# Encoder trunk on one core: x added group by group, scales and sinks loaded in the first network, two activation buffers asked for later, two norm buffers for four blocks

## Chip, cores, metric

The kernel runs on one core of one Trainium2 chip. The metric is the device time of one execution in microseconds (us), taken as the median of several runs. One profiled execution gives the trace from which all lines below come; times in it are counted from the start of its span.

## What is computed

Two layers (DEPTH = 2) of an encoder over 512 tokens of width 1024, each with four sublayers, all in float32, and each ended by a layer norm over the sum with its input:

```python
ALPHA = (2.0 * DEPTH) ** 0.25
for i in range(DEPTH):
    j = i // 2
    y = swiglu(x, ffn_w_gate[i, 0], ffn_w_up[i, 0], ffn_w_down[i, 0])
    x = layer_norm(ALPHA * x + 0.5 * y, ln_g[i, 0], ln_b[i, 0])
    if i % 2 == 0:
        y = mixer_ab(x, ab_w_in[j], ab_w_out[j], ab_q_gain[j], ab_k_gain[j], ab_sink[j], ang_2d, ang_1d)
    else:
        y = mixer_c(x, c_w_in[j], c_w_out[j], c_rpb[j])
    x = layer_norm(ALPHA * x + y, ln_g[i, 1], ln_b[i, 1])
    y = memory_attn(x, mem, mem_w_q[i], mem_w_kv[i], mem_w_o[i])
    x = layer_norm(ALPHA * x + y, ln_g[i, 2], ln_b[i, 2])
    y = swiglu(x, ffn_w_gate[i, 1], ffn_w_up[i, 1], ffn_w_down[i, 1])
    x = layer_norm(ALPHA * x + 0.5 * y, ln_g[i, 3], ln_b[i, 3])
```

`swiglu` is `(silu(x @ w_gate) * (x @ w_up)) @ w_down` with 2816 hidden features. In `mixer_ab`, q and k of the A heads are RMS-normed with a learned scale (`ab_q_gain`, `ab_k_gain`, 64 numbers each) before a rotary embedding, and the B heads have one learned sink logit each (`ab_sink`).

## The kernel before

**Stages.** `run` calls eight stages in order: network 0 (`ffn(0)`), `mixer_ab`, `memory(0)`, networks 1 and 2 (`ffn(1)`, `ffn(2)`), `mixer_c`, `memory(1)`, network 3. The 512 tokens lie in four blocks of 128 rows, `self.x[0]` to `self.x[3]`, each [128, 1024]; the same values transposed and split in two float32r parts are `xh` and `xl`. Every matmul is three products of such parts (`mm3`): high by high, high by low, low by high. So each weight is loaded, its high half is made by a cast on ScalarE (ACT) and its low half by a subtraction on VectorE (DVE); that is `split`.

**A network.** `ffn` works in groups of 512 hidden features. Group 0 is done plainly: 256 features by `ffn_by_features` (network 0) or `ffn_by_tokens` (the others), 256 by `hidden`. Groups 1 to 4 (`hidden_steps`, `down_steps`) use Strassen's seven products. In group g the steps of the hidden layer of g are interleaved with the steps of the down projection of group g-1, 28 steps in all, and `pipeline` loads for a step three steps ahead and splits its weights one step ahead. The down products come in the order (1, 6, 2, 5, 3, 7, 4), each for two token blocks b; products 2 and 3 add into blocks 0 and 1, products 5, 7 and 4 into blocks 2 and 3, on VectorE. Some sums of weights are made by a second load that adds onto the first (`plus`, an accumulating DMA on POOL's queue). The last 256 features come at the end (`finish`), block by block, with the norm of each block.

In network 0 the first down products write the x tiles instead of adding to them, and the input x itself is added by an accumulating DMA of 512 KB per block on POOL's queue (`add_x`). All four are asked for after group 1, in `after_first`, where the masks (`band`, `near`) are loaded too.

**The norm.** `layer_norm(t, ...)` has sums of the rows from the last additions; VectorE makes the negative mean `nmu` and `y = (x + nmu) * g`, ScalarE the sum of squares (`var`, written beside `junk`), POOL the reciprocal root in two operations (`rsqrt`, tile `lny`), VectorE the end, `x = y * r + b`. Then TensorE transposes the block and `split` makes `xh` and `xl`.

**The first mixer's start.** `mixer_ab` loads three rotary tables, `rope_2d` twice and `rope_1d`, into slabs, and the scales of q into the tile `gain` by three DMAs, and POOL multiplies the q table by them in four operations. The scales of k go through the same tile (one buffer) into the k table. The sinks are loaded after that and negated on VectorE. All these loads are on SP's queue, behind the last load of the network (`nc.after`).

**Buffers.** Weights, their halves, activations, norm buffers, `ln_g` and `ln_b` share one pool of 27 slabs of 4 KB per partition. `raw` has two buffers of 8 KB. PSUM has banks a (3), d (2), t (3).

**The order.** Nothing is run when it is written down: `Graph` records all operations with their dependencies, and `emit` plans each engine's order at build time with its own costs (`cost`) and issues them so. An operation is ready when what it depends on is done and its buffers are granted. Among the ready ones of an engine the one that was recorded first goes first, with a short patience on VectorE and ScalarE. A pool's buffers are granted strictly in the order in which they were asked for, whichever is used first. On the chip each engine then works in that fixed order, and a waiting instruction holds up all behind it. All recorded instructions carry line 143.

The central lines of the buffers' order:

```python
        def grant(space):

            while space.next < len(space.queue) and space.free:
                info = space.queue[space.next]
                space.next += 1
```

Of the kernel before, what the change touches and what calls it, by code (L numbers as in the profile page):

```python
# [17 lines left out]
ALU = mybir.AluOpType  # L18
# [234 lines left out]
class Kernel:  # L253
# [118 lines left out]
    def rsqrt(self, sums, n, tag, mean, eps):  # L372

        nc = self.nc
        y = self.small(n, tag + "y")
        nc.gpsimd.tensor_scalar(y, sums, mean, eps, ALU.mult, ALU.add)
        nc.gpsimd.tensor_tensor(out=y, in0=y, in1=self.nhalf[:, :n], op=ALU.pow)
        return y
# [32 lines left out]
    def layer_norm(self, t, st, gb, last):  # L411

        nc = self.nc
        g, b = gb
        x = self.x[t]
        halves = [(0, 512), (512, D)] if last and t == NT - 1 else [(0, D)]
        nmu = self.small(1, "nmu")
        nc.vector.tensor_scalar(nmu, st[:, 0:1], st[:, 1:2], -1.0 / D, ALU.add, ALU.mult)
        var = self.small(1, "var")
        y = self.slab(F32)  # L420
# [19 lines left out]
    def down(self, acts, wts, coef, ln=None, blocks=range(NT)):  # L440
# [3 lines left out]
        for t in blocks:  # L444
            st = self.small(2, "st") if ln else None
# [41 lines left out]
    def ffn_by_features(self, wg, wu, dst):  # L487
# [9 lines left out]
        for lo, hi in steps:  # L497
# [10 lines left out]
            for k in range(lo, hi):  # L508
                for parts, pair in zip(got, banks):
                    for b, ps in enumerate(pair):  # L510
                        st = [z[:, k % 4, b * P : (b + 1) * P] for z in parts[k // 4]]
                        self.mm3(ps, st, self.xT(k, 0, S), k == 0, k == KB - 1)
        for b in range(2):
            self.gated(banks[0][b], banks[1][b], dst=dst[:, :, b, :])

    def ffn_by_tokens(self, wg, wu, dst):
# [3 lines left out]
        for t in range(NT):  # L520
# [7 lines left out]
            sgs.append(self.gated(*both, 256))  # L528
        for b in range(2):
            ps = self.transposed([(t * P, P, sgs[t][:, b * P : (b + 1) * P]) for t in range(NT)])  # L530
            self.nc.scalar.copy(dst[:, :, b, :], ps.rearrange("p (s n) -> p s n", s=2))

# [22 lines left out]
    def hidden(self, wg, wu, c0, dst=None):  # L555

        gate, up = self.w_halves(wg, c0), self.w_halves(wu, c0)
        got = []
        for b in range(2):
# [4 lines left out]
            got.append(self.gated(pg, pu, dst=None if dst is None else dst[:, :, b, :]))  # L564
        return got
# [194 lines left out]
    def ffn(self, i, ln_i, last, aside=None):  # L760
# [8 lines left out]
        hs[0].extend(self.slab(F32, (P, 2, 2, 256)) for _ in range(2))  # L769
        if i == 0:  # L770
            self.ffn_by_features(wg, wu, hs[0][0])
        else:
            self.ffn_by_tokens(wg, wu, hs[0][0])
        self.hidden(wg, wu, groups[0][1], hs[0][1])
        xs = self.token_sums()

        def after_first():
            if i == 0:
                for t in range(NT):
                    self.add_x(t)  # L780
            if aside:
                nc.after = [op for op in nc.ops if op.dma and op.engine == "sync"][-1], {"sync"}
                aside()
                nc.after = None

        steps = []
        for g in range(1, 5):
# [5 lines left out]
            if g == 1:  # L793
                steps.append(only(after_first))
        tail, wt, ln, ws = [], {}, {}, []
# [109 lines left out]
    def mixer_ab(self, ln_i, last):  # L905
# [14 lines left out]
        for name, gain in (("q", "ab_q_gain"), ("k", "ab_k_gain"), ("b", None)):  # L920
# [5 lines left out]
            if gain:  # L926
                gn = self.small(128, "gain", 1)
                nc.sync.dma_start(out=gn[:, 0:64], in_=a[gain][0:1, :].broadcast_to([P, 64]))
                for h in range(2):
                    nc.sync.dma_start(  # L930
                        out=gn[:, 64 + 32 * h : 96 + 32 * h],
                        in_=a[gain][0:1, 32 - 32 * h : 64 - 32 * h].broadcast_to([P, 32]),
                    )
                for t in range(NT):
                    nc.gpsimd.tensor_tensor(out=tab[:, t, :], in0=tab[:, t, :], in1=gn, op=ALU.mult)
            tabs[name] = tab
        nsink = self.small(8, "nsink", 1)
        nc.sync.dma_start(out=nsink, in_=a["ab_sink"][0:1, :].broadcast_to([P, 8]))
        nc.vector.tensor_scalar(nsink, nsink, -1.0, None, ALU.mult)
# [487 lines left out]
    def masks(self):  # L1427
# [3 lines left out]
        self.nc.sync.dma_start(out=self.near, in_=self.a["near"])  # L1431

# [99 lines left out]
```

## Time and profile before

| | us |
|---|---|
| median of 3 runs (lowest, highest) | 2179.78 (2179.76, 2180.21) |
| the profiled execution | 2181.09 |
| its span, first to last instruction | 2179.3 |

The mean granted TensorE clock is 0.993 of full speed. DMA queues moved 273.89 MB; 13.3% of the 16 DMA engines' time went to the software queue (POOL's), 32.8% to the hardware queue (SP's and ACT's).

A line of a timeline has the start, the length of the merged piece, the engine, the operation, out<-in by tile names, the count, and in brackets the engine's idle time before it and what ended that. A line of the chain of waits has start, length, what. PE is TensorE's matmul, PEld its weight load, SPq the sequencer of SP, which issues most loads. A row on DMA issues has the tile, the queue, the count, KB each and the median time from issue to landing.

### The profile page before, as it was taken

What the parts mean: (1) busy time and instruction counts of PE and PEld (TensorE: products, weight loads), DVE (VectorE), ACT (ScalarE), POOL (GpSimd) and SP (SyncE); (2) the same over time, 40 slices, a digit from 0 to 9 for tenths busy, and PEclk for the clock granted to TensorE, in tenths of its full rate; (3) what the DMA queues carried; (4) which work ended last, traced back from release to release, by engine and by line L of the source; (5) the groups of instructions that cost most, each with busy time, mean ns of one, the idle gap of its engine ahead of it and who ended that gap; (6) DMA issues with size and microseconds to landing.
All of it is one profiled execution on the core that took longest, in us unless ns stands there. A gap on an engine that the chain in (4) does not pass through costs nothing.

```text
span 2179.3 us, 33960 instructions
## 1 busy us (share of the span) xinstructions
PE 2135.5 (98%) x13408; PEld 1923.0 (88%) x13408; DVE 1726.6 (79%) x2461; ACT 1066.8 (49%) x1671; POOL 350.6 (16%) x467
## 2 busy tenths in 40 slices
PE   9999999999999999999999999999999999999997
PEld 7989987778898899999789999888989989999996
DVE  7789987788755868999778999867677558699996
ACT  5545443467443544545435455445554435445552
POOL 0010013544000000000200001304330000000002
PEclk9999999999999999999999999999999999999999
DMA  6665552102442346556335555545553423465552
GB/s 194 165 144 138 141 180 73 32 11 70 134 135 88 97 116 179 142 136 164 107 82 141 146 135 141 155 117 149 147 164 117 135 88 98 116 148 146 134 155 67
DMA packets 210575, 273.89 MB, mean 126 GB/s; under 512 B 10481, under 2 KB 159601, under 8 KB 210417
## 3 DMA queue, kind: packets, MB, share of 16 engines
q1 hardware_dynamic: 178704, 221.14, 32.8%
q0 software_dynamic: 31424, 50.34, 13.3%
q8 instruction: 105, 1.72, 0.3%
q14 instruction: 54, 0.43, 0.1%
q10 hardware_dynamic: 288, 0.26, 0.0%
HBM read 257.02 MB, written 4.19 MB: 120 GB/s over the span
## 4 chain that ended last, share of the span: by engine, by line
PE 91%; DVE 3%; DMA 2%; ACT 1%; POOL 1%; issue 1%; SPq 1%; DVEq 0%; POOLq 0%; ACTq 0%
PE a L143 56%; PE d L143 21%; PE t L143 13%; DVE slab L143 2%; DVE x L143 1%; DVE t L143 1%; ACT slab L143 1%; POOL slab L143 1%; SPq L143 1%; DMA slab<-ffn_w_down 0%; DMA slab<-ffn_w_up 0%; DMA raw<-ab_w_out 0%; ACT t L143 0%; DMA gain<-ab_k_gain 0%; ACT junk L143 0%
## 5 line engine op out<-in xcount | busy, mean ns | idle before, releaser
L143 DVE TENSOR_TENSOR slab<-slab,slab 128x1024 fp32r<-128x1024 f32 (+3 forms) x614 | 696.9, 1163 | 50.0 <-ACT slab L143 27.2
L143 ACT CAST slab<-slab 128x1024 fp32r<-128x1024 f32 (+2 forms) x478 | 456.8, 984 | 322.9 <-DVE slab L143 138.6
L143 PE MATMUL a<-slab,slab 128*128 128x256 f32 (+3 forms) x2744 | 590.6, 307 | 2.4 <-ACT t L143 1.1
L143 PE MATMUL a<-xh,slab 128*128 128x256 f32 (+2 forms) x2480 | 559.2, 314 | 1.6 <-ACT slab L143 1.6
L143 PEld LDWEIGHTS a<-slab,slab 128*128 128x128 f32 x2744 | 447.7, 191 | 35.8 <-DVE slab L143 5.0
L143 PE MATMUL d<-slab,slab 128*128 128x512 f32 (+2 forms) x1856 | 453.4, 383 | 4.2 <-ACT slab L143 2.9
L143 PEld LDWEIGHTS a<-xh,slab 128*128 128x128 f32 x2480 | 416.5, 190 | 34.7 <-ACT slab L143 2.1
L143 PE MATMUL a<-raw,slab 128*128 128x256 f32 x2048 | 390.2, 283 | 4.0 <-DVE t L143 4.0
L143 PE MATMUL a<-xl,slab 128*128 128x256 f32 (+1 forms) x1240 | 390.1, 315 | 0.0
L143 PEld LDWEIGHTS d<-slab,slab 128*128 128x128 f32 x1856 | 329.0, 189 | 60.6 <-ACT slab L143 4.5
L143 PEld LDWEIGHTS a<-raw,slab 128*128 128x128 f32 x2048 | 329.1, 192 | 9.2 <-issue 4.4
L143 PEld LDWEIGHTS a<-xl,slab 128*128 128x128 f32 x1240 | 236.1, 190 | 17.6
L143 PE MATMUL t<-slab,slab 128*128 128x512 f32 (+1 forms) x792 | 193.3, 383 | 2.6 <-ACT slab L143 1.5
L143 DVE TENSOR_TENSOR slab<-raw,slab 128x1024 fp32r<-128x1024 f32 (+2 forms) x140 | 171.5, 1242 | 19.8 <-ACT slab L143 19.2
L143 PEld LDWEIGHTS t<-slab,slab 128*128 128x128 f32 x792 | 137.7, 189 | 26.8 <-issue 2.5
L143 ACT CAST slab<-t 128x512 fp32r<-128x512 f32 (+2 forms) x205 | 110.2, 563 | 96.2 <-PE t L143 66.8
L143 POOL TENSOR_TENSOR t<-t,l 128x256 f32<-128x256 f32 (+2 forms) x104 | 84.5, 833 | 369.2 <-DVE l L143 368.7
L143 ACT CAST slab<-raw 128x1024 fp32r<-128x1024 f32 (+1 forms) x132 | 131.8, 1026 | 22.6 <-DMA raw<-mem_w_kv 8.6
L143 DVE TENSOR_TENSOR slab<-t,slab 128x512 fp32r<-128x512 f32 (+2 forms) x205 | 127.8, 646 | 17.0 <-ACT slab L143 16.5
L143 DVE SCALAR_TENSOR_TENSOR x<-d,x 128x512 f32<-128x512 f32 x164 | 111.7, 687 | 34.1 <-PE d L143 33.6
L143 ACT COPY t<-a 128x512 f32<-128x512 f32 x96 | 56.3, 586 | 160.5 <-PE a L143 89.2
L143 POOL DMA_DIRECT2D slab<-ffn_w_down x40 | 47.8, 1194 | 306.7 <-DVE slab L143 273.7
(124 smaller groups left out, 2218.3 us busy)
## 6 DMA issues: line engine op xcount, KB each, us to landing
slab<-ffn_w_gate SPq DMA_DIRECT2D x86, 512.0 KB
slab<-ffn_w_up SPq DMA_DIRECT2D x86, 512.0 KB
slab<-ffn_w_down SPq DMA_DIRECT2D x80, 512.0 KB
slab<-ffn_w_down POOLq DMA_DIRECT2D x40, 512.0 KB, 6.0
slab<-t SPq DMA_DIRECT2D x96, 128.0 KB
slab<-ffn_w_gate POOLq DMA_DIRECT2D x16, 512.0 KB, 6.0
slab<-ffn_w_up POOLq DMA_DIRECT2D x16, 512.0 KB, 5.9
raw<-mem_w_kv SPq DMA_DIRECT2D x8, 1024.0 KB
```

The source lines that it names most:

```text
L143: op.call = lambda: fn(*args, **kw)
```

## The change

The input x is no longer added to all four blocks after group 1: block 0 is added after group 1, blocks 1 to 3 in groups 2 to 4, as a step of its own, eight steps ahead of the group's end. The scales of q and of k get a tile each, and they and the sinks (negated) are loaded in `masks`, that is, in network 0's `after_first`; the multiplications of the tables stay in `mixer_ab`. The two activation buffers of group 0 are asked for where they are first written (`new()`), behind the requests for the weights that come before. `layer_norm` keeps two norm buffers, used in turn by the four blocks, in the list `gb`, in place of one per block. The small tiles of the sums and roots have 4 buffers in place of 8.

```diff
@@ -372,7 +372,7 @@
     def rsqrt(self, sums, n, tag, mean, eps):
 
         nc = self.nc
-        y = self.small(n, tag + "y")
+        y = self.small(n, tag + "y", 4)
         nc.gpsimd.tensor_scalar(y, sums, mean, eps, ALU.mult, ALU.add)
         nc.gpsimd.tensor_tensor(out=y, in0=y, in1=self.nhalf[:, :n], op=ALU.pow)
         return y
@@ -411,13 +411,17 @@
     def layer_norm(self, t, st, gb, last):
 
         nc = self.nc
-        g, b = gb
+        g, b = gb[:2]
         x = self.x[t]
         halves = [(0, 512), (512, D)] if last and t == NT - 1 else [(0, D)]
-        nmu = self.small(1, "nmu")
+        nmu = self.small(1, "nmu", 4)
         nc.vector.tensor_scalar(nmu, st[:, 0:1], st[:, 1:2], -1.0 / D, ALU.add, ALU.mult)
-        var = self.small(1, "var")
-        y = self.slab(F32)
+        var = self.small(1, "var", 4)
+        if len(gb) < 3:
+            gb.append([])
+        if len(gb[2]) < 2:
+            gb[2].append(self.slab(F32))
+        y = gb[2][t % 2]
         nc.vector.scalar_tensor_tensor(out=y, in0=x, scalar=nmu, in1=g, op0=ALU.add, op1=ALU.mult)
         nc.scalar.activation(self.junk, x, AF.Square, bias=nmu, scale=1.0, accum_out=var)
         r = self.rsqrt(var, 1, "ln", 1.0 / D, LN_EPS / ALPHA**2)
@@ -442,7 +446,7 @@
         nc = self.nc
         n = len(acts)
         for t in blocks:
-            st = self.small(2, "st") if ln else None
+            st = self.small(2, "st", 4) if ln else None
             for h in range(2):
                 ps = self.ps("da"[h])
                 for i in range(n):
@@ -484,7 +488,7 @@
         for i in range(n):
             nc.tensor.matmul(ps, zero[:, :P], zero, start=i == 0, stop=i == n - 1)
 
-    def ffn_by_features(self, wg, wu, dst):
+    def ffn_by_features(self, wg, wu, new):
 
         nc = self.nc
         self.warm(8)
@@ -510,10 +514,12 @@
                     for b, ps in enumerate(pair):
                         st = [z[:, k % 4, b * P : (b + 1) * P] for z in parts[k // 4]]
                         self.mm3(ps, st, self.xT(k, 0, S), k == 0, k == KB - 1)
+        dst = new()
         for b in range(2):
             self.gated(banks[0][b], banks[1][b], dst=dst[:, :, b, :])
-
-    def ffn_by_tokens(self, wg, wu, dst):
+        return dst
+
+    def ffn_by_tokens(self, wg, wu, new):
 
         gate, up = self.w_halves(wg, 0), self.w_halves(wu, 0)
         sgs = []
@@ -526,9 +532,11 @@
                     self.mm3(ps[:, :256], self.xT(k, t * P, (t + 1) * P), mv, k == 0, k == KB - 1)
                 both.append(ps[:, :256])
             sgs.append(self.gated(*both, 256))
+        dst = new()
         for b in range(2):
             ps = self.transposed([(t * P, P, sgs[t][:, b * P : (b + 1) * P]) for t in range(NT)])
             self.nc.scalar.copy(dst[:, :, b, :], ps.rearrange("p (s n) -> p s n", s=2))
+        return dst
 
     def quarter(self, w, q, c):
 
@@ -552,17 +560,18 @@
     def w_halves(self, w, c0):
         return [self.wide(self.quarter(w, q, c0)) for q in range(2)]
 
-    def hidden(self, wg, wu, c0, dst=None):
+    def hidden(self, wg, wu, c0, new):
 
         gate, up = self.w_halves(wg, c0), self.w_halves(wu, c0)
-        got = []
+        dst = None
         for b in range(2):
             pg, pu = self.ps("a"), self.ps("a")
             for ps, w in ((pg, gate), (pu, up)):
                 for k in range(KB):
                     self.mm3(ps, [z[:, k % 4, b * P : (b + 1) * P] for z in w[k // 4]], self.xT(k, 0, S), k == 0, k == KB - 1)
-            got.append(self.gated(pg, pu, dst=None if dst is None else dst[:, :, b, :]))
-        return got
+            dst = dst or new()
+            self.gated(pg, pu, dst=dst[:, :, b, :])
+        return dst
 
     def token_sums(self):
 
@@ -766,18 +775,12 @@
         none = lambda: None
         only = lambda f: (none, none, f)
         hs = [[] for _ in groups]
-        hs[0].extend(self.slab(F32, (P, 2, 2, 256)) for _ in range(2))
-        if i == 0:
-            self.ffn_by_features(wg, wu, hs[0][0])
-        else:
-            self.ffn_by_tokens(wg, wu, hs[0][0])
-        self.hidden(wg, wu, groups[0][1], hs[0][1])
+        new = lambda: self.slab(F32, (P, 2, 2, 256))
+        hs[0].append((self.ffn_by_tokens if i else self.ffn_by_features)(wg, wu, new))
+        hs[0].append(self.hidden(wg, wu, groups[0][1], new))
         xs = self.token_sums()
 
         def after_first():
-            if i == 0:
-                for t in range(NT):
-                    self.add_x(t)
             if aside:
                 nc.after = [op for op in nc.ops if op.dma and op.engine == "sync"][-1], {"sync"}
                 aside()
@@ -792,6 +795,8 @@
                 steps += [p, q] if q else [p]
             if g == 1:
                 steps.append(only(after_first))
+            if i == 0:
+                steps.insert(len(steps) - 8 if g > 1 else len(steps), only(lambda t=g - 1: self.add_x(t)))
         tail, wt, ln, ws = [], {}, {}, []
         for b in range(2):
             for name, w in (("gate", wg), ("up", wu)):
@@ -924,19 +929,10 @@
             for t in range(NT):
                 nc.sync.dma_start(out=tab[:, t, :], in_=src.rearrange("(r c) d -> c r d", c=GRID_W)[16 * t : 16 * t + 16])
             if gain:
-                gn = self.small(128, "gain", 1)
-                nc.sync.dma_start(out=gn[:, 0:64], in_=a[gain][0:1, :].broadcast_to([P, 64]))
-                for h in range(2):
-                    nc.sync.dma_start(
-                        out=gn[:, 64 + 32 * h : 96 + 32 * h],
-                        in_=a[gain][0:1, 32 - 32 * h : 64 - 32 * h].broadcast_to([P, 32]),
-                    )
                 for t in range(NT):
-                    nc.gpsimd.tensor_tensor(out=tab[:, t, :], in0=tab[:, t, :], in1=gn, op=ALU.mult)
+                    nc.gpsimd.tensor_tensor(out=tab[:, t, :], in0=tab[:, t, :], in1=self.gains[name], op=ALU.mult)
             tabs[name] = tab
-        nsink = self.small(8, "nsink", 1)
-        nc.sync.dma_start(out=nsink, in_=a["ab_sink"][0:1, :].broadcast_to([P, 8]))
-        nc.vector.tensor_scalar(nsink, nsink, -1.0, None, ALU.mult)
+        nsink = self.nsink
         nc.after = None
 
         def proj(ps, t, w, ks=range(KB)):
@@ -1429,6 +1425,18 @@
         self.nc.sync.dma_start(out=self.band, in_=self.a["band"])
         self.near = self.tile(self.cst, [P, 3, 32], F32, "near")
         self.nc.sync.dma_start(out=self.near, in_=self.a["near"])
+        self.gains = {}
+        for name in "qk":
+            gn, src = self.small(128, "gain" + name, 1), self.a[f"ab_{name}_gain"][0:1, :]
+            self.nc.sync.dma_start(out=gn[:, 0:64], in_=src.broadcast_to([P, 64]))
+            for h in range(2):
+                self.nc.sync.dma_start(
+                    out=gn[:, 64 + 32 * h : 96 + 32 * h], in_=src[:, 32 - 32 * h : 64 - 32 * h].broadcast_to([P, 32])
+                )
+            self.gains[name] = gn
+        self.nsink = self.small(8, "nsink", 1)
+        self.nc.sync.dma_start(out=self.nsink, in_=self.a["ab_sink"][0:1, :].broadcast_to([P, 8]))
+        self.nc.vector.tensor_scalar(self.nsink, self.nsink, -1.0, None, ALU.mult)
 
     def run(self, phases=8):
         nc, a = self.nc, self.a
```

## The prediction

> **What bounds the kernel now.** I read the page first, then the busy time in windows, the longest pieces of the chain of waits, and the timelines around them.
>
> ```profile
> PE 2135.5 (98%) x13408; PEld 1923.0 (88%) x13408; DVE 1726.6 (79%) x2461; ACT 1066.8 (49%) x1671; POOL 350.6 (16%) x467
> ```
>
> TensorE is busy 98% of the span, so nothing is gained by making another engine's work shorter in general. What can be gained is where TensorE stands still, and what follows: after a long enough stop the clock is granted at half. The windows around four stops (columns: start:end, length, busy time of PE, PEld, DVE, ACT, POOL, granted clock, DMA share, GB/s; the fifth is for comparison):
>
> ```profile
> 133.64:137.05 3.41, 3.41 (x19) 3.41 (x18) 3.38 (x5) 0.69 (x2) 0.00 (x0) 0.50 0.02 5
> 341.85:348.68 6.83, 5.28 (x17) 4.50 (x18) 6.54 (x9) 4.19 (x6) 2.04 (x4) 0.50 0.02 7
> 389.64:393.05 3.41, 3.41 (x10) 2.63 (x9) 3.08 (x12) 0.28 (x2) 2.06 (x4) 0.50 0.44 129
> 1085.96:1096.20 10.24, 7.14 (x32) 6.68 (x33) 9.39 (x11) 7.36 (x13) 1.97 (x2) 0.50 0.17 51
> ```
> ```profile
> 862.00:869.00 7.00, 5.40 (x35) 4.53 (x34) 5.93 (x7) 4.55 (x6) 1.19 (x1) 1.00 0.60 182
> ```
>
> Work done at 0.50 costs half of its busy time extra. The last row is the counterexample: 1.6 us idle, clock kept. The stops themselves, from TensorE's timeline (idle before the instruction in brackets):
>
> ```profile
> 133.31 0.36 PE L143 MATMUL a<-raw,slab 128*128 128x256 f32 x1 [3.97 <-DVE t L143]
> ```
> ```profile
> 337.84 0.39 PE L143 MATMUL a<-slab,slab 128*128 128x512 f32 x1
> 343.40 1.97 PE L143 MATMUL t<-ident,x 128*128 128x128 f32 x8 [5.18 <-DVE x L143]
> ```
> ```profile
> 388.74 0.33 PE L143 MATMUL t<-ident,slab 128*128 128x128 f32 x1 [1.83 <-POOL slab L143]
> ```
> ```profile
> 1086.79 1.94 PE L143 MATMUL t<-ident,x 128*128 128x128 f32 x8 [2.91 <-DVE x L143]
> ```
> ```profile
> 1091.41 0.88 PE L143 MATMUL t<-ident,x 128*128 128x128 f32 x3 [2.28 <-DVE x L143]
> ```
>
> Stop A, in group 1 of the first network: 3.97 + 3.41/2 = 5.7 us. Stop B, between that network and the first mixer: 5.18 + 5.28/2 = 7.8 us. Stop C, between the two networks in the middle: 2.91 + 2.28 + 7.14/2 = 8.8 us. The change touches all three.
>
> **The change part by part.**
>
> *x added group by group.* Stop A ends a load of up weights that took 10.72 us (chain of waits), while the software queue (POOL) carried the additions of x:
>
> ```profile
> 116.55 2.89 PE a L143 x24
> 119.46 10.72 DMA slab<-ffn_w_up
> ```
> ```profile
> 109.61 2.26 POOL L143 DMA_DIRECT2D x<-x  x2
> ```
> ```profile
> slab<-ffn_w_down POOLq DMA_DIRECT2D x2, 512.0 KB, 12.6
> ```
> ```profile
> slab<-ffn_w_down POOLq DMA_DIRECT2D x2, 512.0 KB, 6.4
> ```
>
> The last two rows are the median time to landing of the same accumulating weight loads, from 104 to 124 us (group 1) and from 169.5 to 189.5 us (group 2, where no x is added). The four up loads leave alike in both groups, but only the first group's are late:
>
> ```profile
> 119.46 10.27 SPq L143 DMA_DIRECT2D slab<-ffn_w_up  x4
> ```
> ```profile
> 184.79 10.27 SPq L143 DMA_DIRECT2D slab<-ffn_w_up  x4
> ```
> ```profile
> 104.00:124.00 20.00, 20.00 (x146) 18.91 (x145) 17.02 (x20) 8.85 (x12) 5.46 (x5) 1.00 0.93 208
> 169.50:189.50 20.00, 20.00 (x144) 18.91 (x144) 20.00 (x25) 11.09 (x14) 3.67 (x3) 1.00 0.66 139
> ```
>
> 208 against 139 GB/s over 20 us is 1.4 MB more, of which the two additions (512 KB each) are 1.0 MB. After the change blocks 2 and 3 are added in groups 3 and 4, so group 1 meets group 2's conditions. To remove the stop the critical load must land by 130.18 - 3.97 = 126.2 us, in 6.7 us instead of 10.7; without 1.0 MB in front, at the 208 GB/s of the row, it gains 5.0 us. I take the whole 5.7 us; the low end is 0, if the load is late for another reason.
>
> Each later group gets one addition. It starts when the block's last write in that group before it is done and must land before the next one. For block 1 in group 2 these are, on VectorE, and the landing time of the four additions of today (shortest, median, longest):
>
> ```profile
> 143.96 0.68 DVE L143 SCALAR_TENSOR_TENSOR x<-d,x 128x512 f32<-128x512 f32 x1
> ```
> ```profile
> 160.64 0.69 DVE L143 SCALAR_TENSOR_TENSOR x<-t,x 128x512 f32<-128x512 f32 x1
> ```
> ```profile
> DMA to landing us min/median/max: 6.8/9.7/13.0
> ```
>
> 160.64 - 143.96 - 0.68 = 16.0 us of room against 13.0 at worst. Blocks 2 and 3 have the same four steps of room in groups 3 and 4 by the order of the steps (5 then 7). If an addition were late, VectorE would wait in order, with the weight splits queued behind it. I put 0 here; upper bound 13.0 us of VectorE wait in one group, if the addition left 16 us late.
>
> *Scales and sinks loaded early.* Stop B is a queue in order. The scales of k share one buffer with those of q, so their load (SP) waits for POOL's last multiplication by the scales of q, and POOL then waits for the load with the norm's square root behind it:
>
> ```profile
> 333.42 1.28 SPq L143 DMA_DIRECT2D gain<-ab_k_gain  x3
> ```
> ```profile
> 331.53 1.87 POOL L143 TENSOR_TENSOR slab<-slab,gain 128x128 f32<-128x128 f32 x2
> 339.42 1.27 POOL L143 TENSOR_TENSOR slab<-slab,gain 128x128 f32<-128x128 f32 x3 [6.03 <-DMA gain<-ab_k_gain]
> 340.79 0.18 POOL L143 TENSOR_SCALAR lny<-var 128x1 f32<-128x1 f32 x1
> 341.05 0.45 POOL L143 TENSOR_TENSOR slab<-slab,gain 128x128 f32<-128x128 f32 x1
> 341.46 0.57 POOL L143 TENSOR_TENSOR lny<-lny,nhalf 128x1 f32<-128x1 f32 x1
> ```
> ```profile
> 335.21 0.19 ACT L143 ACTIVATION_READ_ACCUMULATOR junk<-x,nmu 128x1 f32 x1
> ```
> ```profile
> 342.06 1.28 DVE L143 SCALAR_TENSOR_TENSOR x<-slab,lny,slab 128x1024 f32<-128x1024 f32 x1 [5.40 <-POOL lny L143]
> ```
>
> The variance is there at 335.40. From the root's first step to VectorE's took 342.06 - 340.79 = 1.27 us, 0.45 of it a multiplication put between, so 0.82; from there to TensorE 343.40 - 342.06 = 1.34. With POOL free the transposes could start at 335.40 + 0.82 + 1.34 = 337.6, before TensorE's last product ends at 338.2: no stop. If all four multiplications for k stand ahead at 1.87/2 = 0.94 us each, POOL is free at 333.40 + 3.74 = 337.1 and the stop is 337.1 + 0.82 + 1.34 - 338.2 = 1.1 us. I take 0.6 between the two. Either is under the 1.6 us that left the clock alone, so the half clock goes too: 7.8 - 0.6 = 7.2 us. Low end 3 us, if the weights' splits, which shared the stop, become the bound.
>
> The Trainium skill (TensorE: Matmul & The Clock Gate, Part 1 and "HAM oscillation") says that the clock is halved after an idle window of some 3.4 us. This trace halves it after 1.83 us too (388.74 and the row from 389.64), so the measurement decides; by the page C's gaps would not have halved the clock, and C would be worth 5.2 us.
>
> What is added for it: seven small loads in group 1, on SP, at the median of three:
>
> ```profile
> 103.29 0.42 SPq L143 DMA_DIRECT2D near<-near  x1
> 106.58 6.12 SPq L143 DMA_DIRECT2D slab<-ffn_w_down  x2
> ```
> ```profile
> 289.07 1.53 SPq L143 DMA_DIRECT2D gain<-ab_q_gain  x3
> ```
>
> 7 x 0.51 = 3.6 us of issues in a hole of 106.58 - 103.71 = 2.9 us: the next load, of down weights, leaves 0.7 us late, and the one behind it waits for most of the row's 6.12 us anyway. What hides it is TensorE's run without a stop up to 129; without that it costs 0.7. By bytes they are 132 KB (128 rows of 512 B twice, and of 32 B) where 1.5 MB leave. VectorE's negation of the sinks, 8 elements, waits in order for the last of the seven; 0 if landed, at worst a load's landing: the k scales took 339.42 - 334.70 = 4.7 us from the end of their issues to POOL's start. I take 0, since VectorE has 3 us of slack in the 20 us of the first 104.00 row.
>
> The Trainium skill (DMA: Bandwidth & Descriptors, Specifications) speaks against these: transfers under 512 B per row don't reach line rate. At four times their bytes they would be an estimated 0.5 MB, still a third of what leaves.
>
> *Activation buffers later, norm buffers two for four.* All slabs (27) are granted in the order of request. In the middle transition the requests of two norm and two activation buffers stand ahead of the next network's weights; they go.
>
> ```profile
> 1055.96 2.86 SPq L143 DMA_DIRECT2D slab<-ffn_w_gate  x2
> ```
> ```profile
> 1072.59 4.36 SPq L143 DMA_DIRECT2D slab<-ffn_w_up  x2
> ```
> ```profile
> 1075.27 1.27 DVE L143 SCALAR_TENSOR_TENSOR x<-slab,lny,slab 128x1024 f32<-128x1024 f32 x1
> ```
> ```profile
> 1091.18 2.36 DVE L143 TENSOR_TENSOR slab<-slab,slab 128x1024 fp32r<-128x1024 f32 x2
> ```
>
> The two gate loads of the first row leave within 2.86 us and stand three requests apart (a raw slab and the two of its split), so four requests are about 2.86 x 4/3 = 3.8 us. That doesn't by itself close stop C: the first low half of the new weights is made at 1091.18, 35 us after the load, because VectorE is taken by the sums and norms that the plan ranks first. Bounds: 0, if the low halves stay there, and all 8.8. One low half made ahead frees 24 of the 96 products of blocks 0 and 1 that could fill the stop, 2.9 us by the row of 24 above (116.55). I take 3.0, nearest to that one half. In the first network the 26 slabs up to the first activation buffers are free at the start, so nothing moves there; elsewhere I put 0, as TensorE doesn't stop at those transitions. The smaller buffers of the sums and roots (4 for 8) serve four blocks each: 0.
>
> **Sum.** 5.7 + 7.2 + 3.0 = 15.9 us. The profiled execution took 2181.09 us (span 2179.3), so 2165.2; the median of the runs is 1.3 lower, hence **2163.9 us**.
>
> **Rivals.** *The up load is late for itself* (its slab, not the additions): the change doesn't do what part one says. For it: the load leaves SP only at 119.46, 6.7 us before it is needed. Against: group 2's row. A and C stay, 2179.8 - 7.2 = 2172.6.
>
> *Stop C goes whole*: 5.7 + 7.2 + 8.8 = 21.7, 2158.1. For: weights 3.8 us earlier. Against: VectorE's order.
>
> *Slower: the two norm buffers are held from the first block to the last.* Today a norm's slab returns with its block; the second load of the 1072.59 row leaves just when the norm of 1075.27 ends. If the next stage runs out of the other 25 slabs between block 0 and block 3, its weights come late at up to seven transitions. At B's price, 7.8 us, three such stops outweigh A and B: 2179.8 - 12.9 + 23.4 = 2190.3; it decides from two on. Against: two requests disappear as well.
>
> *No change*: the order of instructions is planned anew for the whole kernel, and stops like the 1.83 us one, with 1.7 us of half clock (3.5 together), arise four times in the mixers: 2179.8 - 15.9 + 14 = 2177.9.
>
> **Chances.** Forecast 0.52 (own range 2158 to 2169), late load 0.13, C whole 0.13, no change 0.12, slower 0.10. A change of 0.2% (4.4 us) is what the measurement can tell. Faster 0.52 + 0.13 + 0.13 = 0.78, same 0.12, slower 0.10. The range, 2155 to 2179, leaves out the slower case and the edges.
>
> **What would show it.** In the changed profile: A right, if group 1's accumulating loads land in some 6 us and no stop over 1 us lies near 130; B right, if POOL runs from the scales' multiplications to the root without a wait for a DMA, and TensorE's stop near 335 is under 1.5 us at full clock; C, if a low half is made before the last norms. Wrong, if VectorE waits for x<-x in groups 2 to 4, or SP's loads at the transitions leave later than now.

## The result and the profile after

The changed kernel takes 2163.71 us (median of 6 runs, 2161.99 to 2164.34), the kernel before 2179.99 us beside it on the same chip (6 runs, 2179.58 to 2184.89): a ratio of 0.9921, 95% interval 0.9908 to 0.9933, or 16.3 us less. The forecast was 2163.9. The profiled execution of the changed kernel took 2164.34 us (span 2162.3, mean granted clock 0.997). Its page, first the engines:

```profile
PE 2130.8 (99%) x13408; PEld 1918.5 (89%) x13408; DVE 1727.5 (80%) x2461; ACT 1066.0 (49%) x1671; POOL 346.8 (16%) x467
```

The number of instructions is the same on every engine. TensorE is busy 4.7 us less (2135.5 before), since less of its work ran at half clock; the rest of the gain is standing still that went. The same places as before, in the windows of the changed kernel (the fifth is the place where the clock is now halved, in `mixer_c`):

```profile
133.64:137.05 3.41, 3.41 (x25) 3.15 (x24) 3.38 (x5) 1.39 (x2) 0.00 (x0) 1.00 0.26 90
341.85:348.68 6.83, 6.83 (x33) 5.57 (x32) 6.29 (x13) 2.00 (x3) 1.65 (x3) 1.00 0.00 0
374.00:381.00 7.00, 4.33 (x22) 3.10 (x20) 6.67 (x16) 1.75 (x5) 4.74 (x5) 1.00 0.18 46
1074.00:1080.00 6.00, 4.59 (x36) 3.98 (x34) 6.00 (x7) 4.49 (x9) 1.98 (x2) 1.00 0.31 87
1420.17:1423.58 3.41, 3.41 (x17) 3.41 (x18) 2.71 (x3) 0.00 (x0) 0.65 (x2) 0.50 0.28 77
```

Both kernels issue the same 13408 products, so the time at which the k-th product ends can be compared in the two traces. Nearly all stand in the same order; near stop C and in `mixer_ab` some do not, so the row of stop C is read together with the row behind it (from the 6285th to the 6640th product, which hold the same work in both kernels, the gain is 7.48 us). Where the difference (before less after) moves by more than 0.45 us, worked out from all of TensorE's instructions:

```
place                                   gain, us   forecast
start of the program                      -1.98       0
stop A, group 1 of network 0              +5.72       5.7
stop B, network 0 to mixer_ab             +7.55       7.2
inside mixer_ab                           +0.52       0
stop C, network 1 to network 2            +8.15       3.0
just behind it                            -0.64       0
entry of mixer_c                          -1.48       0
smaller steps together                    -0.8        0
all, first to last product               +17.0       15.9
```

So the total is right, and two of its terms. The third was 4.5 us too small (7.5 found), and losses that the sum had at nothing hid that.

**A.** TensorE's timeline of the changed kernel, where the 3.97 us stop was: it goes from the six transposing products into the next ones without idle time.

```profile
129.76 1.55 PE L143 MATMUL t<-slab,slab 128*128 128x512 f32 x6
131.15 0.28 PE L143 MATMUL a<-raw,slab 128*128 128x256 f32 x1
```

The four additions of x, now spread over four groups, land sooner (shortest, median, longest; 6.8, 9.7 and 13.0 before):

```profile
DMA to landing us min/median/max: 5.8/6.2/7.1
```

The accumulating weight loads of group 1 (104 to 124 us) land in 7.0 us in place of 12.6, where some 6 were named as the sign:

```profile
slab<-ffn_w_down POOLq DMA_DIRECT2D x2, 512.0 KB, 7.0
```

**B.** POOL's timeline: the tables are multiplied without a wait for a load, and the norm's root follows at once.

```profile
327.77 1.87 POOL L143 TENSOR_TENSOR slab<-slab,gainq 128x128 f32<-128x128 f32 x2
329.61 2.70 POOL L143 TENSOR_TENSOR slab<-slab,gaink 128x128 f32<-128x128 f32 x4
332.40 0.18 POOL L143 TENSOR_SCALAR lny<-var 128x1 f32<-128x1 f32 x1
332.66 0.57 POOL L143 TENSOR_TENSOR lny<-lny,nhalf 128x1 f32<-128x1 f32 x1
```

The transposes of x, which waited 5.18 us, now have no bracket (TensorE):

```profile
334.15 0.39 PE L143 MATMUL a<-slab,slab 128*128 128x512 f32 x1
334.61 1.09 PE L143 MATMUL t<-ident,x 128*128 128x128 f32 x8
```

**C.** On VectorE one low half of network 2's first weights is made at 1053.86, ahead of the norms; before, the first was at 1091.18, behind them.

```profile
1053.86 1.21 DVE L143 TENSOR_TENSOR slab<-slab,slab 128x1024 fp32r<-128x1024 f32 x1
```

TensorE has that half's products to run while the last norms are made; of 2.91 and 2.28 us idle, three short gaps of together 1.40 are left:

```profile
1075.34 1.06 PE L143 MATMUL t<-ident,x 128*128 128x128 f32 x8 [0.73 <-DVE x L143]
1076.64 0.50 PE L143 MATMUL a<-slab,xh 128*128 128x256 f32 x2 [0.24 <-ACT xh L143]
1077.58 0.39 PE L143 MATMUL a<-slab,xh 128*128 128x256 f32 x1 [0.43 <-DVE slab L143]
```

### The profile page after: what moved, and what is told of

Its sections match the earlier page's. It is cut to its first block, busy times and chain, and to the rows that moved or that the text cites. A ratio compares the mean times of both kernels' runs of the same rounds, so it can differ in the third digit from the quotient of the medians.

```text
span 2162.3 us, 33929 instructions
## 1 busy us (share of the span) xinstructions
PE 2130.8 (99%) x13408; PEld 1918.5 (89%) x13408; DVE 1727.5 (80%) x2461; ACT 1066.0 (49%) x1671; POOL 346.8 (16%) x467
## 4 chain that ended last, share of the span: by engine, by line
PE 91%; DVE 4%; POOL 1%; ACT 1%; DMA 1%; issue 1%; SPq 0%; DVEq 0%; POOLq 0%; ACTq 0%
PE a L143 57%; PE d L143 21%; PE t L143 13%; DVE slab L143 2%; DVE t L143 1%; DVE x L143 1%; ACT slab L143 1%; POOL slab L143 1%; DMA slab<-ffn_w_down 1%; POOL x L143 0%; ACT t L143 0%; DMA raw<-ab_w_out 0%; ACT junk L143 0%; POOL lny L143 0%; POOL rms8y L143 0%
```

## The experiments

Ratios are to the kernel before, measured in turns with it on the same chip. Executions of one kernel differ by several us (before: 2177.5 to 2186.0 in the first group of runs), so the parts are judged by their traces first, and by the totals second. A gain at a place is the step in the product-by-product difference to before's trace, as in the table.

### Stop A

**The additions alone** (`e1_x_groups`):

```diff
         def after_first():
-            if i == 0:
-                for t in range(NT):
-                    self.add_x(t)
...
+            if i == 0:
+                steps.insert(len(steps) - 8 if g > 1 else len(steps), only(lambda t=g - 1: self.add_x(t)))
```

> Part one alone, on the kernel before: x added group by group. Theory (the four additions of x crowd the DMA engines in group 1): TensorE's stop of 3.97 us near 129 and the half clock behind it go, so the time falls by 5.7 us, from 2180.0 to about 2174.3; the accumulating down-weight loads of group 1 land in about 6 us instead of 12.6. The stops near 338 (5.18 us) and near 1087 (2.91 and 2.28 us) stay. Rival (the up load is late because its slab comes late): the stop stays over 3 us and the time within 1 us of before.

2177.63 us (2173.8 to 2181.63), ratio 0.9982, 0.9971 to 0.9992. The gain at A is 4.11 us, not 5.7. The chain of waits and TensorE's line behind it:

```profile
119.48 8.11 DMA slab<-ffn_w_up
```
```profile
130.72 0.35 PE L143 MATMUL a<-raw,slab 128*128 128x256 f32 x1 [1.36 <-DVE t L143]
```

The up load got faster (10.72 to 8.11 us), by 2.6 of the 4.0 us that were needed (6.7). The accumulating down loads land in 8.3 us, not in the expected 6. What is left, 1.36 us, is short enough that the clock stays: 3.97 - 1.36 idle and 1.7 of half clock are 4.3, about the step measured. The stops at B (5.20 us) and C (2.91 and 2.28) stand. That stop A varies by itself is seen in the four kernels whose group 1 is untouched (`e2_k_tile`, `e3_hs_late`, `e4_two_norms`, `e7_hs_and_norms`): the up load takes 9.9 to 11.5 us, and 3.1 to 4.7 us of stop remain.

**All four additions after group 2** (`e5_x_after_2`), so that group 1 carries none:

```diff
+            if g == 2 and i == 0:
+                steps.append(only(lambda: [self.add_x(t) for t in range(NT)]))
```

> All four additions of x at once, but after group 2 instead of after group 1, on the kernel before. Theory (crowding by the additions): the stop near 129 goes and a stop of 2 to 4 us with a late up load appears one group later, near 189; the time stays within 3 us of before. Rival (the stop belongs to group 1, whatever is added there): it stays near 129, and none appears near 189.

2178.01 us (2175.68 to 2180.59), ratio 0.9984, 0.9975 to 0.9993; gain at A 3.85 us. The chain of waits:

```profile
119.36 8.38 DMA slab<-ffn_w_up
```

With no x in group 1 at all the load still takes 8.4 us, and 1.64 us of stop remain. So the additions are not what keeps it from 6.7 us; what does is seen in the next pair of runs. And with all four additions in that group (the last leaves at 172.39 and lands 12.0 us later), group 2 does not stop. Its up loads on SP, and ScalarE's wait for the first:

```profile
180.85 4.51 SPq L143 DMA_DIRECT2D slab<-ffn_w_up  x2
```
```profile
189.64 2.00 ACT L143 CAST slab<-slab 128x1024 fp32r<-128x1024 f32 x2 [2.98 <-DMA slab<-ffn_w_up]
```

The load lands 8.7 us after it leaves, and TensorE still has work past that: group 2 has more time for it than the 6.7 us of group 1. Without the additions it does not need that time: in the kernel before, the same load of group 2, at 184.79, lands in 3.9 us.

**The additions and the early scales, without the buffer edits** (`e8_x_and_early`), and **everything but the early scales** (`e9_no_early`: loads at the mixer's start as before, but a tile each for q and k). The edits, against the changed kernel:

```diff
-        y = gb[2][t % 2]
+        y = self.slab(F32)
...
-        new = lambda: self.slab(F32, (P, 2, 2, 256))
+        hs[0].extend(self.slab(F32, (P, 2, 2, 256)) for _ in range(2))
```
```diff
             if gain:
+                gn = self.small(128, "gain" + name, 1)
+                nc.sync.dma_start(out=gn[:, 0:64], in_=a[gain][0:1, :].broadcast_to([P, 64]))
...
-        self.gains = {}
...
```

> The changed kernel without its buffer edits: additions of x group by group, scales of q and k and the sinks loaded in the first network. The additions alone left 1.36 us of the stop near 129. If the early small loads shift the order of group 1 and take that rest away: stop near 129 at most 0.3 us, the up load's last issue and landing no longer the end of a wait, A worth 5.7. If the rest hangs on the buffer edits: 1.36 again. The stop between network 0 and the mixer gone under both (7.5 us), the 2.91 + 2.28 between the two middle networks left under both. Total under the first: 2180 - 5.7 - 7.5 = 2167; under the second: 2180 - 4.1 - 7.5 = 2168.5; the trace tells them apart, not the total.

> The changed kernel with the scales and the sinks loaded where they were before, at the mixer's start, but q's and k's scales in a tile of their own each. If the shared tile was the whole of the stop before the mixer, it stays gone (under 0.3 us idle near 335) and early loading is worth nothing there. If the early loads were needed for the first group: a stop of about 1.36 us near 129 is back; if not, that stop is at most 0.3. Total 2163.7 under the latter, about 2165.3 under the former. The middle transition keeps its gain of 8 us under both.

`e8_x_and_early`: 2170.44 us (2169.02 to 2171.69), ratio 0.9952, 0.9937 to 0.9967. No idle time near 129, gain at A 5.71; B 7.54; C's two gaps stand (2.90 and 2.29). `e9_no_early`: 2164.38 us (2163.17 to 2164.58), ratio 0.9923, 0.9907 to 0.994. B 7.53, C 8.15, and at A only 4.07, with the short stop back. Its TensorE and ScalarE lines, and the chain of waits:

```profile
132.59 0.36 PE L143 MATMUL a<-raw,slab 128*128 128x256 f32 x1 [1.41 <-DVE t L143]
```
```profile
129.53 2.00 ACT L143 CAST slab<-slab 128x1024 fp32r<-128x1024 f32 x2 [3.37 <-DMA slab<-ffn_w_up]
```
```profile
121.30 8.15 DMA slab<-ffn_w_up
```

The last 1.4 to 1.6 us of A thus come from the small loads of scales and sinks, which were meant for another place. Two pairs of runs show it, `e1_x_groups` with `e8_x_and_early` and `e9_no_early` with the changed kernel. What they do is seen on SP, first in the kernel without them (`e9_no_early`), then in the changed kernel:

```profile
99.18 0.47 SPq L143 DMA_DIRECT2D slab<-ffn_w_down  x1
108.42 6.11 SPq L143 DMA_DIRECT2D slab<-ffn_w_down  x2
```
```profile
99.09 1.48 SPq L143 DMA_DIRECT2D gainq<-ab_q_gain  x3
100.61 3.31 SPq L143 DMA_DIRECT2D gaink<-ab_k_gain  x3
104.13 0.33 SPq L143 DMA_DIRECT2D nsink<-ab_sink  x1
105.80 0.38 SPq L143 DMA_DIRECT2D slab<-ffn_w_down  x1
```

They hold SP for 5.4 us, a down load leaves 6.6 us later, and the plan orders group 1 differently. What changes for the up load is what goes just ahead of it. The up loads (SP) and the last accumulating down load of the group (POOL), in `e9_no_early`, then in the changed kernel:

```profile
121.30 10.27 SPq L143 DMA_DIRECT2D slab<-ffn_w_up  x4
120.55 1.20 POOL L143 DMA_DIRECT2D slab<-ffn_w_down  x1 [5.23 <-DVE slab L143]
```
```profile
121.43 10.27 SPq L143 DMA_DIRECT2D slab<-ffn_w_up  x4
123.62 1.20 POOL L143 DMA_DIRECT2D slab<-ffn_w_down  x1 [6.53 <-DVE slab L143]
```

In the first the accumulating load leaves 0.7 us ahead of the first up load, in the second 2.2 us behind it. Then the up load lands in 4.1 us (by its landing events in the trace, at 125.55), ScalarE's cast of it at 126.19 waits for nothing, and so none of the casts from 126 to 134 waits for an up load. While the up load was under way, the software queue, which carries the accumulating loads, moved 0.52 MB in `e9_no_early` (121.30 to 129.46) and 0.11 MB in the changed kernel (121.43 to 125.55).

All twelve traces go by this order: in the eight with the accumulating load ahead, the up load takes 8.1 to 11.5 us; in the four with it behind, all of which have the early small loads, 3.8 to 4.1. In group 2 of the kernel before it is behind as well (186.20 against 184.79), and the load took 3.9.

That the early loads bring the better order is shown by the pairs of runs; no run moved the accumulating load alone, so the order as the cause is read from the traces and not isolated, and whether SP's time or any other shift makes such a plan was not tried. The early loads also have a price: the plan orders `mixer_ab` differently with them, and a stop of 1.83 us there (1.82 in `e9_no_early`) is 2.56 in the changed kernel. In the total the difference can't be told: 2164.38 and 2163.71 have overlapping intervals.

### Stop B

**A tile each for the scales, loaded where they were** (`e2_k_tile`; the small tiles at 4 buffers make the room):

```diff
-                gn = self.small(128, "gain", 1)
+                gn = self.small(128, "gain" + name, 1)
```

> A tile of its own for the scales of k on the kernel before, with the small tiles at 4 buffers, which makes the room; the loads stay at the mixer's start. Theory (the wait is for the shared tile): SP issues the k scales right behind those of q and the sinks, POOL no longer waits for a DMA, TensorE's stop near 338 falls from 5.18 us to under 1.1 and the half clock of 6.83 us behind it goes: 7.5 us less, about 2172.5. Rival (the early place in network 0 is what matters, since the loads at the mixer's start are behind the tables): POOL still waits over 3 us for the k scales, and the time falls by less than 3 us.

2173.68 us (2171.52 to 2175.68), ratio 0.9965, 0.9952 to 0.9978, and 7.53 us gained at B. POOL:

```profile
332.61 1.86 POOL L143 TENSOR_TENSOR slab<-slab,gainq 128x128 f32<-128x128 f32 x2
334.44 2.70 POOL L143 TENSOR_TENSOR slab<-slab,gaink 128x128 f32<-128x128 f32 x4
337.23 0.18 POOL L143 TENSOR_SCALAR lny<-var 128x1 f32<-128x1 f32 x1
```

One shared tile was the whole of B. Loading the scales of k some 190 us earlier (100.61 in the changed kernel, 291.87 here) adds nothing there. (This profiled execution lost 1.2 us more at A than before's: the up load took 11.46 us, and 6.83 us at half clock followed in place of 3.41.)

### Stop C

**The activation buffers alone** (`e3_hs_late`), **the norm buffers alone** (`e4_two_norms`), **both** (`e7_hs_and_norms`):

```diff
-        hs[0].extend(self.slab(F32, (P, 2, 2, 256)) for _ in range(2))
...
+        new = lambda: self.slab(F32, (P, 2, 2, 256))
+        hs[0].append((self.ffn_by_tokens if i else self.ffn_by_features)(wg, wu, new))
+        hs[0].append(self.hidden(wg, wu, groups[0][1], new))
```
```diff
-        y = self.slab(F32)
+        if len(gb[2]) < 2:
+            gb[2].append(self.slab(F32))
+        y = gb[2][t % 2]
```

> Only the two activation buffers of group 0 asked for later, on the kernel before. Theory (two slabs less ahead of the next network's weights): the first gate load of network 2 leaves about 1.9 us earlier than 1055.96 against the same point of the stage, half of what both buffer edits do; if that is enough for one low half ahead of the norms, the stop near 1087 falls from 5.2 us to about 1.4 and its half clock goes, 8 us less (2172); if not, the stop and the time stay within 1 us. Rival (the norm buffers do it alone): time and stop as before.

> Only two norm buffers for four blocks, on the kernel before. Theory (each pair of slabs counts alike): as for the activation buffers, the first gate load of network 2 leaves about 1.9 us earlier; 8 us less if a low half is made ahead of the norms, else within 1 us. Rival (buffers held from the first block to the last starve the next stage): stops of over 2 us appear at the transitions, and the time rises by 5 us or more.

> Both buffer edits, without the other two parts, on the kernel before. Theory (four slabs ahead of the weights let one low half be made before the norms): the stop near 1087 falls from 5.2 to about 1.4 us without half clock behind it, 8 us less: 2172. The stops near 129 and 338 stay as they are. Rival (the gain in the middle comes from the earlier parts, by another order of the plan): the stop near 1087 stays over 4 us.

```
                  median (lowest to highest)     ratio                     gain at C
e3_hs_late        2175.78 (2172.87 to 2179.90)   0.9976 [0.9966, 0.9986]   8.13
e4_two_norms      2174.84 (2171.26 to 2178.14)   0.9968 [0.9959, 0.9978]   8.14
e7_hs_and_norms   2173.97 (2173.20 to 2175.90)   0.9965 [0.9950, 0.9979]   8.14
```

Either edit alone wins this step, and both together win no more. Over the 6285th to the 6640th product the three gain 7.5, 9.1 and 7.5 us: in `e4_two_norms` the last gaps, of 1.4 us, are gone too. The medians show less of it, 5.2, 6.2 and 8.0 us against before's of the same group of runs. `e4_two_norms` also settles the slower rival: with only two norm buffers no transition got a new stop.

Two requests less ahead of the weights are thus enough, but not in the way that was expected. The loads do not leave earlier, by 1.9 us or at all: in all twelve traces the first gate load of network 2 leaves 0.03 us after the 6355th product ends. In the changed kernel:

```profile
1044.51 0.37 SPq L143 DMA_DIRECT2D slab<-ffn_w_gate  x1
```

What comes earlier is the low half. ScalarE's cast of that load, before, then after:

```profile
1060.73 1.05 ACT L143 CAST slab<-slab 128x1024 fp32r<-128x1024 f32 x1 [4.14 <-DMA slab<-ffn_w_gate]
```
```profile
1049.12 1.05 ACT L143 CAST slab<-slab 128x1024 fp32r<-128x1024 f32 x1 [3.99 <-DMA slab<-ffn_w_gate]
```

VectorE makes the low half 30.5 us later before (1091.18) and 4.7 us later after (1053.86). That its slab is granted sooner fits the order of the requests; no run shows the grants themselves.

### Versions beyond the change

Two stops of the changed kernel are the one of 2.56 us in `mixer_ab` behind POOL and one in network 1, where ScalarE is late while sixteen tables are copied at once (TensorE, changed kernel):

```profile
853.98 0.50 PE L143 MATMUL t<-slab,slab 128*128 128x512 f32 x1 [1.54 <-ACT slab L143]
```

**The tables copied four after each of groups 1 to 4** (`e6_bias_spread`):

```diff
             if g == 1:
                 steps.append(only(after_first))
+            if later:
+                steps.append(only(lambda part=g - 1: queued(part)))
```

> On the changed kernel, the same idea for the 16 bias tables that network 1 copies from DRAM to DRAM after its group 1: four after each of groups 1 to 4. Theory (they crowd group 1 of that network as the additions of x did): the stop of 1.54 us near 852 goes, and the time falls by about 1.5 us, 2163.7 to 2162.2; it had no half clock behind it. Rival (the down load there is late for another reason): the stop and the time stay.

2159.83 us (2158.41 to 2160.76), ratio 0.9896, 0.9881 to 0.9911; the stop is gone, and the trace gains 1.19 and 0.92 us there, more than the 1.5 expected. The rest of the distance to 2163.71 is not shown to be its doing: the start of the program is 2.1 us shorter in this execution and the half clock of `mixer_c` is missing (1.5), while 1.1 us are lost at C.

**Besides, the plan's price for a root on POOL** (`e10_root_cost`). The plan counted 500 ns; in the changed kernel the operation took 1.64 us for 8 values per row, and TensorE's transpose stands behind it:

```profile
371.00 1.64 POOL L143 TENSOR_TENSOR rms8y<-rms8y,nhalf 128x8 f32<-128x8 f32 x1
374.84 2.17 POOL L143 TENSOR_TENSOR slab<-t,t 128x512 f32<-128x512 f32 x1 [2.20 <-DVE t L143]
```
```profile
377.07 0.33 PE L143 MATMUL t<-ident,slab 128*128 128x128 f32 x1 [2.56 <-POOL slab L143]
```

```diff
         if n <= 8:
-            return 270.0 if method == "tensor_scalar" else 500.0
+            return 270.0 if method == "tensor_scalar" else 420.0 + 155.0 * n
```

> The kernel with network 1's sixteen bias tables copied four after each of groups 1 to 4, and besides the planner's cost of a GpSimd root set to 420 + 155 n ns in place of 500 (the traces have 1.64 us for 8 values a row, 0.70 for 2, 0.55 for 1). If the mixer's stops before its transposes (2.56, 0.89 and 1.11 us in the changed kernel, all behind GpSimd) come from the root being planned three times too short: they shrink by 1 to 3 us, total 2157 to 2159. If the order of GpSimd is set by data and not by the cost: same stops, total 2159.8. A new order for the whole kernel may also open stops elsewhere: 2160 to 2163.

2156.79 us (2155.11 to 2157.83), ratio 0.9889, 0.9874 to 0.9904. The stop is 1.08 us in its TensorE timeline, and against the changed kernel's trace the mixer gains 1.47 + 1.51 - 0.57 = 2.4 us:

```profile
376.90 0.33 PE L143 MATMUL t<-ident,slab 128*128 128x128 f32 x1 [1.08 <-POOL slab L143]
```

This is the fastest kernel of the study, 24.0 us under the 2180.8 of the kernel before in the same group of runs. Its interval overlaps that of `e6_bias_spread`; that the mixer's part is real rests on the traces. Whether the truer price is needed for it, or another order of the plan would do the same, was not tried.

## Why the prediction came out

**A, 5.7 forecast, 5.72 found: right sum, partly wrong reason.** The additions do crowd the up load, and to spread them is worth 4.1 us. The step that failed is "so group 1 meets group 2's conditions". It took the bytes of the two groups as the whole difference. The order differs too: in group 1 an accumulating down load leaves just ahead of the up load, in group 2 behind it. With the additions spread or gone and this order kept (`e1_x_groups`, `e5_x_after_2`, `e9_no_early`), group 1 needs the load in 6.7 us and gets it in 8.1 to 8.4. The other 1.6 us came from the early small loads, a term that the sum had at 0, and with a guard on the wrong side: the next load was to leave 0.7 us late, it left 6.6 us late, the accumulating load went behind the up load, and that helped. The sign "no stop over 1 us near 130" was met for a reason that was not foreseen. What the same loads cost in `mixer_ab`, 0.7 us of stop, stood at 0 as well.

**The additions in later groups, 0 forecast: right.** The room was 16.0 us, the longest landing 7.1. In VectorE's instructions on x in groups 2 to 4 no idle time ends with x<-x.

**B, 7.2 forecast, 7.55 found: right, cause and size.** The stop of 0 to 1.1 us that was left open came out at 0, though by the second of the two orders: all four multiplications for k stood ahead of the root, but took 2.70 us instead of 3.74, so that POOL was free in time. The cause, the shared tile, is shown by `e2_k_tile`; of the edit's two halves, tile and place, only the tile does it.

**C, 3.0 forecast, 8.15 found (7.5 with the row behind it): right effect, size far off, and a step on the way wrong.** The forecast was that one low half is made ahead, and one is. But it was to come of weights that leave 3.8 us earlier, and they leave no earlier; that failed without harm, since the low half alone counts. The step that was mis-sized is "frees 24 of the 96 products ... 2.9 us": it counted the idle time that these products fill, and left out what follows from filling it. Idle fell from 5.19 to 1.40 us, 3.8, and no window then was idle enough to halve the clock, so the 7.14/2 = 3.6 us of half-clock work went as a whole: together 7.4 of the 7.5. That the clock stays is not sure at this stop: in `e6_bias_spread`, whose three gaps there are the same (0.74, 0.24 and 0.44), 1.41 us of idle time fell together and 3.41 us at half clock followed, and the same stretch of products gained 6.4 us. The upper bound of 8.8 had the two together; the value taken in between had no such jump in it. The rival *stop C goes whole* was nearer here.

**Two losses the sum had at 0** made up for that. At the start of the program the same products, in the same order, run at half pace for longer in the changed kernel's execution. Before, then after (TensorE's timeline):

```profile
6.31 0.39 PE L143 MATMUL a<-xl,slab 128*128 128x512 f32 x1
```
```profile
6.41 0.63 PE L143 MATMUL a<-xl,slab 128*128 128x512 f32 x1
```

That costs 1.98 us, and 1.85 to 2.09 in `e9_no_early`, `e3_hs_late`, `e7_hs_and_norms` and `e10_root_cost`, but nothing in `e8_x_and_early` and the rest; the products and their order are the same there in all twelve traces, and `e6_bias_spread` has every edit of the changed kernel, so it is put down to the execution and not to the kernel. At `mixer_c` the clock is halved where it was not before, although the gaps are the same there. Before, then after:

```profile
1436.12 1.06 PE L143 MATMUL t<-ident,x 128*128 128x128 f32 x8 [0.99 <-DVE nmu L143]
1437.96 0.51 PE L143 MATMUL a<-slab,xh 128*128 128x256 f32 x2 [0.77 <-ACT xh L143]
```
```profile
1417.46 1.06 PE L143 MATMUL t<-ident,x 128*128 128x128 f32 x8 [0.98 <-DVE nmu L143]
1419.29 0.50 PE L143 MATMUL a<-slab,xh 128*128 128x256 f32 x2 [0.77 <-ACT xh L143]
```

Without these 3.5 us of chance the trace would have gained about 20.5. But chance went the other way too. The same stop at B costs 0.7 to 1.1 us less in `e1_x_groups`, `e4_two_norms`, `e5_x_after_2` and `e7_hs_and_norms`, where 3.41 us at half clock follow it and not 6.83; and the stop of 1.83 us in `mixer_ab`, with half clock behind it before, stands without half clock in six other kernels, worth some 1.2 us. So a sum over one pair of traces is good to some 2 us only. The closeness of 2163.71 to 2163.9 is in part luck, as is A's sum; the sign, B's term and the place of C's gain are not.

**The rivals.** *The up load is late for itself* was true for 1.4 to 1.6 us of A in so far as the additions are not the cause of them; the accumulating load ahead of it is what the traces show, not its slab. It did not show in the changed kernel. *Slower by norm buffers* and *no change by new stops of the plan* are refuted by `e4_two_norms` and by the changed trace, where the idle gaps over 0.15 us sum to 18.7 us against 30.8 before.

## What to carry to other kernels

A stop of TensorE has two prices, its idle time and the half-clock time behind it; work that fills part of a stop can win back all of the second, so cost the fill by both. When a load is late in one group and not in another, compare the time at which each is needed and what leaves just ahead of it: the same 512 KB took 8.2 us here with an accumulating load 0.7 us ahead, and 4.1 with it 2.2 us behind. A one-buffer tile that two loads share in turn, on a queue where a norm stands behind, is worth looking for first: a tile of 512 bytes per partition was worth 7.5 us here.

## What was not expected of the hardware

The granted clock changes at points of a fixed grid of 3.413 us, which lies differently in each execution: all changes to half clock in the twelve traces fall on such points counted from the first one recorded (3.93 us in before's execution, 10.46 in the changed kernel's). What decides is the idle time inside one grid window, not the length of a stop. The same transposes of `mixer_ab` waited 2.52 us in `e8_x_and_early` and 2.56 in the changed kernel (both behind POOL). In the first, the idle time fell into one window (372.58, TensorE busy 0.95 of 3.41) and the next ran at half clock; in the second it was split over two (busy 2.25 and 2.03), and the window from 374.00 to 381.00 above has the clock at 1.00 throughout. Windows on the grid, `e8_x_and_early`, then the changed kernel:

```profile
372.58:375.99 3.41, 0.95 (x5) 0.82 (x6) 3.41 (x4) 0.90 (x3) 3.10 (x2) 1.00 0.00 0
375.99:379.41 3.42, 3.42 (x10) 2.64 (x9) 3.09 (x12) 0.27 (x1) 2.07 (x4) 0.50 0.49 123
```
```profile
372.27:375.69 3.42, 2.25 (x13) 1.65 (x12) 2.98 (x5) 1.21 (x2) 1.22 (x2) 1.00 0.00 1
375.69:379.10 3.41, 2.03 (x10) 1.69 (x11) 3.12 (x6) 0.54 (x2) 3.08 (x3) 1.00 0.00 0
```

Over all twelve traces every full-clock window with more than 1.92 us idle was followed by a half-clock one and none with less than 1.41; in between both happen (1.41 at stop C in `e6_bias_spread` and 1.70 at `mixer_c` halved it, 1.76 in `e3_hs_late` did not), and what decides there stays open. The forecast's "1.6 us that left the clock alone" was such a case: 1.46 of it fell into one window. The Trainium skill (TensorE: Matmul & The Clock Gate, Part 1) gives the window as 3413 ns and free-running, and the traces agree; it has the clock fall after a whole idle window, and here 1.70 us of idle time in 3.41, in gaps under 1 us each, did it.

That the executions of one kernel differ by where the grid lies is argued from this and not shown, since no kernel has two traces. Before spans 8.5 us from its fastest to its slowest run in one group, where a half-clock window more or less is up to 1.7 us, and the start up to 2. The mean granted clocks of these 26 runs go along with it: the 7 with 0.991 or 0.992 took 2182.2 us or more, the 11 with 0.994 or more at most 2182.1. In the 7 runs of before beside `e9_no_early` no such order is seen.
